# Indexer tiles of the first half in the first pass, x in reverse, weight sums that hold a block, and a planner rate of 360 GB/s

## The chip, the cores and the metric

The kernel runs on one core of one Trainium2 chip. The metric is the device time of one execution in microseconds; of several runs the median counts. A core has a matrix engine (TensorE, "PE", with its weight loads "PEld"), VectorE ("DVE"), ScalarE ("ACT"), GpSimd ("POOL") and SyncE ("SP"), which issues nearly all DMA transfers of this kernel.

## The reference, cut to what matters

One layer over a sequence of 1024 tokens, model width 2048. One input projection, 6752 columns wide, feeds two groups: sparse attention with a token indexer, and a Mamba-2 state-space mixer. One output projection and a layer norm follow.

```python
u = jnp.einsum('bsd,de->bse', h, w_in[layer])
q, k, v, z_attn, q_idx, k_idx, w_idx, z_ssd, xbc, dt_raw = _split_cols(u, IN_WIDTHS)
...
logits = jax.nn.relu(jnp.einsum('bqhd,bsd->bqhs', qib, k_idx32))      # 16 indexer heads of 64
score = jnp.einsum('bqhs,bqh->bqs', logits, wb)
score = jnp.where(admissible[None], score, -jnp.inf)                  # chunk-causal, chunks of 64
_, sel = lax.top_k(score, topk)                                       # 256 keys for each query
...                                                                   # softmax attention over those keys
mixed = jnp.concatenate([o_attn, o_ssd], axis=-1)
sub = jnp.einsum('bse,ed->bsd', mixed, w_out[layer])
h = _layer_norm(DEEPNORM_ALPHA * h + sub, ln_g[layer], ln_b[layer])
```

The first 256 queries have no more than 256 admissible keys, so the first half of the sequence needs indexer scores only for its last 256 queries (blocks 2 and 3 of 128), the second half for all 512 (blocks 4 to 7).

## The kernel before, in words

**Precision and pieces.** Each fp32 operand is split into a high and a low fp32r part (ScalarE copies the high part, VectorE subtracts: `w_split`, `t_xst`), and a product is three matmuls: high x high, high x low, low x high. The sequence has two halves of 512 tokens (h = 0, 1), the model width two halves of 1024 (u = 0, 1). A piece of the input projection (`Piece`, `emit_t`) multiplies one weight tile of 1024 x 128 by one "set" of x, that is one half h and one width half u, [8 x 128] x 512: 24 matmuls. Indexer tiles ("qi") of h = 0 use only the last 256 columns.

**The plan.** `PLAN` orders the input projection. A tuple (h, tiles, end) is a plain pass: each tile is multiplied by both sets of that half, u = 0 then u = 1. The first three tiles go together (u = 0 for all, then u = 1), then single tiles, then the last `end` tiles together. A list is a group: pairs of tiles go through a Winograd-Strassen scheme with seven products in four phases, over seven sets: x (1,0), the formed sums M2 and M3, x (0,1), the sums S1 and S4, and x (1,1). Sixteen buffers `xh` and sixteen `xl` hold two sets at once. In `units`, a set is requested (`request`, `t_xst`: four DMAs of 512 KB, eight splits) one piece before the set that is two places ahead of it in order of release has had its last use. Before, the order is: pass of h = 0 (5 tiles); pass of h = 1 (13 tiles, all its indexer tiles among them); first group (keys, values, queries); pass of h = 0 over its eight indexer tiles; second group (the rest of the state-space inputs and both gates).

**Tasks.** Everything behind a piece is a Python generator with a priority. `t_qi` rotates an indexer tile, splits it and makes score matmuls for two heads; `t_score` applies ReLU and adds the weighted logits. When all scores of a half are there (`ev_score`), `t_topk` finds the 256th largest by bit-wise search: 32 rounds of ScalarE sign-and-count and three small VectorE operations, for the blocks (2, 3), (4, 5) and (6, 7). Attention (`t_kv`, `t_attn`) runs in the order second half, first half; it needs the masks, and its tiles of the state-space part (`t_ssd`) and the gates run between the pieces. `t_wsum` forms the Strassen sums T1 to T4 of the output weights in DRAM, at priority 5. `t_xform` forms M2, M3, S1 and S4 of x in DRAM.

**The planner.** `Sim` is a model of the engines and of one DMA pipe (`Sim.dma`, L287 and on). At build time it decides which task is emitted next, and so the order of instructions on every queue: a task is emitted when its inputs, by the model, are there, its buffers are free and the clocks of its engines are not too far ahead of TensorE's. All engines then run their queues in that order. `spare_u` is the reserve of `u` buffers that tasks with `keep` leave free. Every instruction goes through one helper, so the profile gives all of them line L313; tiles are told apart by tag: `xt` x in DRAM, `xfM` and `xfS` the formed sums, `xr` and `s` raw x, `wr`, `wh`, `wl` raw, high and low weights, `wo` output weights, `ts` their sums, `pj`, `a`, `o` PSUM tiles, `u` working tiles, `q`, `mask` and `mx` DRAM scratch.

**The output projection** follows as seven products (A11, S3, S1, S2, A22, S4, A12, each eight pieces) over the mixed activations; `forms` and `t_form` load and add their operands. S3 needs the attention outputs of both halves.

Of the kernel before, what the change touches and what calls it, by code (L numbers as in the profile page):

```python
# [13 lines left out]
ALU = mybir.AluOpType  # L14

D = 2048
S = 1024
HALF = 512
P = 128
# [22 lines left out]
def tile_order():  # L42
# [10 lines left out]
FIRST = [("misc", 0), ("xbc", (0, 0)), ("xbc", (0, 1))]  # L53
KVQ = [("k", 0), ("k", 1), ("v", 0), ("v", 1)] + [("q", n) for n in range(8)]
QI = [("qi", j) for j in range(8)]
PLAN = [
    (0, FIRST + [("xbc", (0, 2)), ("xbc", (0, 3))], 2),
    (1, [("misc", 0)] + QI + [("xbc", (0, j)) for j in range(4)], 3),
    [(("k", 0), ("k", 1)), (("v", 0), ("v", 1))] + [(("q", n), ("q", n + 4)) for n in range(4)],
    (0, QI, 3),  # L60
    [(("xbc", (1, j)), ("xbc", (3, j))) for j in range(4)] + [(("xbc", (2, j)), ("xbc", (2, 2 + j))) for j in range(2)]
    + [(("zs", (n // 2, n % 2)), ("z", n)) for n in range(8)],
]
# [60 lines left out]
def in_dram(x):  # L124
    return "DRAM" in str(x.space)
# [6 lines left out]
class Sim:  # L132
# [154 lines left out]
    def dma(self, eng, out, in_, kw):  # L287
        q = {"SP": "SP", "A": "AQ", "G": "G"}[eng]
        lanes = self.lanes["G" if q == "G" else "H"]
        at, notes = self.deps([out], [in_], "D")  # L290
        start = max(self.clk[q], at, lanes.pop(0))
        issue = 1000.0 if eng == "G" else 350.0
        self.clk[q] = start + issue
        sb = in_ if in_dram(out) else out
        row = max(sb.ap[-1][1] * 4, 64)
        x = max(start + issue, self.clk["D"])
        self.clk["D"] = x + max(out.size(), in_.size()) * 4 * (1 / 400 + 0.6 / row)
        cell = [self.clk["D"] + self.LAND, start]
        lanes.append(cell[0])
        self.note(notes, cell, "D")  # L300
        return cell
# [268 lines left out]
class Layer:  # L570
# [20 lines left out]
    def units(self):  # L591

        pieces, work = [], []
        self.hooks = {}
        self.sets = []

        def put(p, listed=True):
            if listed:
                work.append((len(pieces), None))
            pieces.append(p)  # L600
            return len(pieces) - 1

        def plain(h, tile, u, n):
            kind, j = tile
            t = ORDER.index(tile)
            p = Piece("T", h, t, u, load=(("w", t, u),), n=n + u, open=u == 0, close=u == 1, key=(h, t),
                      s0=256 if (kind == "qi" and h == 0) else 0)
            if u == 1:
                p.done = lambda ps: self.fl.add(getattr(self, "t_" + kind)(h, j, ps), 0, f"{kind}{j}h{h}", self.fl.t + 100)
            put(p)  # L610

        for pairs in PLAN:
            if isinstance(pairs, tuple):
                h, tiles, end = pairs
                n = len(self.sets)
                self.sets += [("x", h, 0), ("x", h, 1)]
                for part in [tiles[:3]] + [[t] for t in tiles[3:-end]] + [tiles[-end:]]:
                    for u in range(2):
                        for tile in part:
                            plain(h, tile, u, n)  # L620
                continue
            gi = GROUPS.index(pairs)
            a11 = len(self.sets)
            base = a11 + 1
            self.sets += [("x", 1, 0), ("f", "M2"), ("f", "M3"), ("x", 0, 1), ("f", "S1"), ("f", "S4"), ("x", 1, 1)]
            n = [(a11, base), (base + 1, base + 2), (base + 3, base + 4)]
            couples = [list(range(c, min(c + 2, len(pairs)))) for c in range(0, len(pairs), 2)]
            if len(couples[-1]) == 1:
                couples[-2:] = [couples[-2] + couples[-1]]
            for ph in range(3):  # L630
                for couple in couples:
                    for f in range(2):
                        for c in couple:
                            i = put(self.product(gi, c, pairs[c], ph, f, n[ph][f]))
                            if ph and not (ph == 1 and f == 1):
                                self.hooks.setdefault(max(i - 1, 0), []).append(lambda gi=gi, c=c, ph=ph, f=f: self.pre_ld(gi, c, ph, f))
            for c in range(len(pairs)):
                i = put(self.product(gi, c, pairs[c], 3, 0, base + 5))
                self.hooks.setdefault(i - 1, []).append(lambda gi=gi, c=c: self.pre_ld(gi, c, 3, 0))
        end = {}  # L640
        for i, p in enumerate(pieces):
            end[p.n] = i
        for i in end.values():
            pieces[i].last = True
        freed = sorted(end, key=end.get)
        for n in range(2, len(self.sets)):
            at = end[freed[n - 2]] - 1
            self.hooks.setdefault(at, []).append(lambda n=n: self.request(n))
        self.n_t = len(pieces)
        self.hooks.setdefault(self.n_t - 6, []).append(lambda: self.forms(0))  # L650
        self.hooks.setdefault(12, []).append(self.form_tasks)
        for half in range(2):
            self.hooks.setdefault(12, []).append(lambda half=half: self.fl.add(self.t_wsum(half), 5, "wsum"))
        for n in range(7):
            for d in range(2):
                for j in range(4):
                    if n < 6 or 4 * d + j < 8 - SKEW:
                        work.append((len(pieces), (0, 1, 2, 3)))
                    name = PRODUCTS[n][1]
                    pieces.append(Piece("O", n, d, j, load=(("o", name, d, j),)))  # L660
        for sts in ((0,), (1,), (2,), (3,)):
            work += [(len(pieces) - SKEW + j, sts) for j in range(SKEW)]
        return pieces, work
# [150 lines left out]
    def t_wsum(self, half):  # L814

        fl = self.fl
        cols = slice(512 * half, 512 * half + 512)

        def load(name, d, j):
            x = fl.new("us", [P, 512])  # L820
            fl.dma(x, self.w_block(name, d, j)[:, cols])
            return x

        def save(name, d, j, x):
            fl.dma(self.tsum[name, d, j][:, cols], x)
        for d in range(2):
            for j in range(4):
                yield Need("D", u=2, keep=6)
                x, y = load("B22", d, j), load("B12", d, j)
                yield Need("V")  # L830
                fl.two(x, x, y, ALU.subtract)
                yield Need("D", us=1)
                save("T3", d, j, x)
                fl.free(x)
                z = load("B11", d, j)
                yield Need("V")
                fl.two(y, y, z, ALU.subtract)
                fl.free(z)
                yield Need("D", us=1)
                save("T1", d, j, y)  # L840
                x = load("B22", d, j)
                yield Need("V")
                fl.two(x, x, y, ALU.subtract)
                fl.free(y)
                yield Need("D", us=1)
                save("T2", d, j, x)
                z = load("B21", d, j)
                yield Need("V")
                fl.two(z, x, z, ALU.subtract)
                fl.free(x)  # L850
                yield Need("")
                save("T4", d, j, z)
                fl.free(z)
                fl.signal(self.ev_wsum[half][4 * d + j])
# [641 lines left out]
    def t_score(self, h, i, kh, m, head, r):  # L1496
        fl = self.fl
        yield Need("A")
        fl.act(r[:, 0:m], r[:, 0:m], AF.Relu)
        yield Need("V")  # L1500
        sc = self.score[h][i][:, kh * HALF:kh * HALF + m]
        wcol = getattr(self, f"sd{h}")["wsc"][:, (i - 4 * h) * 16 + head:(i - 4 * h) * 16 + head + 1]
        if head not in self.seen.setdefault((h, i, kh), set()) and not self.seen[h, i, kh]:
            fl.ts(sc, r[:, 0:m], wcol, 0.0, ALU.mult, ALU.add)
        else:
            fl.stt(sc, r[:, 0:m], wcol, sc, ALU.mult, ALU.add)
        self.seen[h, i, kh].add(head)
        fl.free(r)
        self.nlog[h] += 1
        if self.nlog[h] == (32 if h == 0 else 128):  # L1510
            fl.signal(self.ev_score[h])
            if h == 1:
                fl.free(*self.kk[1])
            else:
                fl.free(*self.kk[0])
                fl.spare_u = 4

# [770 lines left out]
```

## Time and profile before

| | |
|---|---|
| median of 3 runs | 1729.61 us (1725.16 to 1730.37) |
| the profiled execution | 1725.14 us, span of its instructions 1723.4 us |
| TensorE busy | 1638.7 us (95%), 8044 matmuls recorded |
| VectorE, ScalarE, GpSimd busy | 1353.0 us (79%), 1019.6 us (59%), 173.5 us (10%) |
| granted TensorE clock, mean | 0.986 |
| DMA | 446.50 MB, mean 259 GB/s |
| `xr<-xt` and `s<-xt`, 512 KB each | 28 and 28 transfers |

Matmuls are pipelined, so a matmul's recorded duration is longer than the distance to the next one; distances between starts are read from the timeline. A wait in square brackets stands behind the instruction that ended it, with what released it. A wait of several causes is put down to the last one.

### The profile page before, as it was taken

To read this page: it belongs to the slowest core of one execution; us is meant where nothing else is said; L and a number is where in the kernel's file an instruction comes from. 1 tells how busy PE (TensorE), PEld (TensorE's weight loads), DVE (VectorE), ACT (ScalarE), POOL (GpSimd) and SP (SyncE) were. 2 spreads that over 40 slices of the span, in tenths; PEclk is the share of its full clock that TensorE was granted. 3 is DMA by queue.
4 is the path that set the end of the run, shared out by engine and by line. 5 is a ranking of instruction groups with operands and counts; after the bars stand their busy time and mean duration, and the time that the engine had idled before them with its cause. 6 is when DMAs were issued, how large, how long until landed. Compare 5 with 4: busy or idle time off the path is not lost. (4 is left out here: it accounts for less than half of the span.)

```text
span 1723.4 us, 24378 instructions
## 1 busy us (share of the span) xinstructions
PE 1638.7 (95%) x8044; PEld 1351.2 (78%) x8044; DVE 1353.0 (79%) x2444; ACT 1019.6 (59%) x1799; POOL 173.5 (10%) x201
## 2 busy tenths in 40 slices
PE   9999999998887989999999999989999999999997
PEld 7877788876666978778888788877888877888875
DVE  5779999787567898789996788845777677659998
ACT  5745575678666856987555478456867544532320
POOL 0000010000000000000222111222121110000110
PEclk9999999999899999999999999999999999999998
DMA  9576578988787678989666875658778999877654
GB/s 320 202 253 230 198 258 290 324 310 307 246 294 259 222 266 271 315 299 318 227 220 219 312 236 188 220 186 251 241 230 280 313 314 342 298 278 268 218 193 147
DMA packets 210215, 446.50 MB, mean 259 GB/s; under 512 B 21928, under 2 KB 61992, under 8 KB 210088
## 3 DMA queue, kind: packets, MB, share of 16 engines
q1 hardware_dynamic: 209656, 444.55, 75.9%
q8 instruction: 63, 1.03, 0.2%
q14 instruction: 64, 0.52, 0.1%
q10 hardware_dynamic: 432, 0.39, 0.1%
HBM read 338.56 MB, written 106.30 MB: 258 GB/s over the span
## 5 line engine op out<-in xcount | busy, mean ns | idle before, releaser
L313 PE MATMUL pj<-xh,wh 128*128 128x512 f32 (+1 forms) x1192 | 470.0, 394 | 25.9 <-ACT wh L313 18.0
L313 PE MATMUL pj<-xh,wl 128*128 128x512 f32 (+1 forms) x1192 | 460.1, 386 | 9.3 <-DVE wl L313 9.1
L313 PE MATMUL pj<-xl,wh 128*128 128x512 f32 (+1 forms) x1192 | 458.8, 385 | 0.1
L313 DVE TENSOR_TENSOR wl<-wr,wh 128x1024 fp32r<-128x1024 f32 (+1 forms) x179 | 213.9, 1197 | 113.2 <-ACT wh L313 112.6
L313 PEld LDWEIGHTS pj<-xh,wh 128*128 128x128 f32 x1192 | 227.1, 191 | 70.7 <-ACT wh L313 20.6
L313 PEld LDWEIGHTS pj<-xh,wl 128*128 128x128 f32 x1192 | 226.5, 190 | 58.8 <-DVE wl L313 14.4
L313 PEld LDWEIGHTS pj<-xl,wh 128*128 128x128 f32 x1192 | 227.3, 191 | 41.2 <-DVE xl L313 1.8
L313 ACT ACTIVATE wh<-wr 128x1024 fp32r<-128x1024 f32 (+1 forms) x185 | 190.6, 1033 | 106.7 <-PE pj L313 67.2
L313 PE MATMUL pj<-xh,s 128*128 128x512 f32 (+1 forms) x688 | 222.1, 385 | 1.8 <-DVE u L313 1.6
L313 PE MATMUL a<-u,u 128*128 128x512 f32 (+3 forms) x746 | 171.7, 351 | 16.4 <-DVE u L313 7.0
L313 PEld LDWEIGHTS a<-u,u 128*128 128x128 f32 x746 | 123.3, 189 | 50.1 <-DVE s L313 10.6
L313 PEld LDWEIGHTS pj<-xh,s 128*128 128x128 f32 x688 | 127.7, 188 | 27.3 <-ACT xh L313 2.3
L313 DVE TENSOR_TENSOR u<-u,u 128x512 f32<-128x512 f32 (+7 forms) x212 | 130.2, 627 | 16.1 <-DMA u<-wo 4.5
L313 ACT ACTIVATE u<-s,sm 128x768 bf16<-128x768 f32 (+7 forms) x132 | 129.6, 982 | 21.3 <-DVE sm L313 19.5
L313 DVE TENSOR_TENSOR wr<-wr,wr 128x1024 f32<-128x1024 f32 (+1 forms) x98 | 121.6, 1243 | 20.5 <-DMA wr<-wt 19.4
L313 ACT ACTIVATE u<-a 128x512 fp32r<-128x512 f32 (+4 forms) x115 | 53.4, 479 | 138.0 <-DVE u L313 66.5
L313 PE MATMUL pj<-xl,s 128*128 128x512 f32 (+1 forms) x344 | 130.8, 380 | 0.8 <-DVE xl L313 0.8
L313 ACT ACTIVATE u<-u 128x512 f32<-128x512 f32 (+4 forms) x165 | 91.9, 566 | 61.5 <-DVE u L313 57.3
L313 ACT ACTIVATE a<-a 128x512 f32<-128x512 f32 (+3 forms) x160 | 76.1, 504 | 70.3 <-PE a L313 69.2
L313 DVE TENSOR_TENSOR s<-wr,s 128x1024 fp32r<-128x1024 f32 (+2 forms) x59 | 70.8, 1200 | 30.7 <-ACT s L313 30.5
L313 DVE TENSOR_TENSOR u<-pj,u 128x512 f32<-128x512 f32 (+2 forms) x94 | 62.4, 664 | 36.7 <-PE pj L313 31.0
L313 PE MATMUL pj<-wh,xh 128*128 128x512 f32 x218 | 87.8, 403 | 1.2 <-DVE u L313 1.2
(253 smaller groups left out, 2678.9 us busy)
## 6 DMA issues: line engine op xcount, KB each, us to landing
wr<-wt SPq DMA_DIRECT2D x228, 512.0 KB, 5.3
u<-u SPq DMA_DIRECT2D x100, 256.0 KB, 5.7
u<-wo SPq DMA_DIRECT2D x79, 256.0 KB, 5.1
wr<-ts SPq DMA_DIRECT2D x32, 512.0 KB, 5.7
ts<-u SPq DMA_DIRECT2D x63, 256.0 KB, 4.3
xr<-xt SPq DMA_DIRECT2D x28, 512.0 KB, 4.9
s<-xt SPq DMA_DIRECT2D x28, 512.0 KB, 6.6
u<-mx SPq DMA_DIRECT2D x49, 256.0 KB, 6.3
```

The source lines that it names most:

```text
L313: f(*args, **kw)
```

## The change

1. The eight indexer tiles of h = 0 stand at the end of the first pass, and the separate pass over them between the two groups is gone. `end` of the first pass is 3 instead of 2.
2. In the pass of h = 1, each tile uses the sets in the order u = 1, u = 0. The first group then begins with (1,0), which is resident, and does not request it again. The second group requests it as before.
3. The first pass's scores and top-k can come before those of the second half. The split keys of h = 0 are freed, and `spare_u` is set to 4, when the scores of both halves are counted (32 + 128 = 160).
4. `t_wsum` loads B22 once and writes T3 into a new buffer; its four subtractions are the same. It asks for three `u` buffers at its start instead of two.
5. The planner's DMA pipe moves 360 instead of 400 bytes per nanosecond.

```diff
 PLAN = [
-    (0, FIRST + [("xbc", (0, 2)), ("xbc", (0, 3))], 2),
+    (0, FIRST + [("xbc", (0, 2)), ("xbc", (0, 3))] + QI, 3),
     (1, [("misc", 0)] + QI + [("xbc", (0, j)) for j in range(4)], 3),
     [(("k", 0), ("k", 1)), (("v", 0), ("v", 1))] + [(("q", n), ("q", n + 4)) for n in range(4)],
-    (0, QI, 3),
...
-        self.clk["D"] = x + max(out.size(), in_.size()) * 4 * (1 / 400 + 0.6 / row)
+        self.clk["D"] = x + max(out.size(), in_.size()) * 4 * (1 / 360 + 0.6 / row)
...
-            p = Piece("T", h, t, u, load=(("w", t, u),), n=n + u, open=u == 0, close=u == 1, key=(h, t),
+            w = u if h == 0 else 1 - u
+            p = Piece("T", h, t, w, load=(("w", t, w),), n=n + u, open=u == 0, close=u == 1, key=(h, t),
...
-                self.sets += [("x", h, 0), ("x", h, 1)]
+                self.sets += [("x", h, h), ("x", h, 1 - h)]
...
             a11 = len(self.sets)
+            if self.sets[-1] == ("x", 1, 0):
+                a11 -= 1
+            else:
+                self.sets.append(("x", 1, 0))
             base = a11 + 1
-            self.sets += [("x", 1, 0), ("f", "M2"), ("f", "M3"), ("x", 0, 1), ("f", "S1"), ("f", "S4"), ("x", 1, 1)]
+            self.sets += [("f", "M2"), ("f", "M3"), ("x", 0, 1), ("f", "S1"), ("f", "S4"), ("x", 1, 1)]
...
-                yield Need("D", u=2, keep=6)
-                x, y = load("B22", d, j), load("B12", d, j)
+                yield Need("D", u=3, keep=6)
+                x, y, z = load("B22", d, j), load("B12", d, j), fl.new("us", [P, 512])
                 yield Need("V")
-                fl.two(x, x, y, ALU.subtract)
+                fl.two(z, x, y, ALU.subtract)
+                yield Need("")
+                save("T3", d, j, z)
+                fl.free(z)
                 yield Need("D", us=1)
-                save("T3", d, j, x)
-                fl.free(x)
                 z = load("B11", d, j)
                 yield Need("V")
                 fl.two(y, y, z, ALU.subtract)
                 fl.free(z)
+                fl.two(x, x, y, ALU.subtract)
                 yield Need("D", us=1)
                 save("T1", d, j, y)
-                x = load("B22", d, j)
-                yield Need("V")
-                fl.two(x, x, y, ALU.subtract)
                 fl.free(y)
-                yield Need("D", us=1)
                 save("T2", d, j, x)
...
             if h == 1:
                 fl.free(*self.kk[1])
-            else:
+            if sum(self.nlog) == 160:
                 fl.free(*self.kk[0])
                 fl.spare_u = 4
```

## The prediction

> **What bounds the kernel now.** I read the page's shares first, then busy time by stage, then the waits of TensorE, then the timeline around the longest one.
>
> ```profile
> span 1723.4 us, 24378 instructions
> PE 1638.7 (95%) x8044; PEld 1351.2 (78%) x8044; DVE 1353.0 (79%) x2444; ACT 1019.6 (59%) x1799; POOL 173.5 (10%) x201
> PEclk9999999999899999999999999999999999999998
> ```
> TensorE is busy 95% of the span, so what an order of work can win is its idle 1723.4 - 1638.7 = 84.7 us, and the time after a pause in which its clock is low. By stage (each row: PE, PEld, DVE, ACT, POOL busy us; granted clock, DMA share, GB/s):
>
> ```profile
> 70.00:246.00 176.00, 170.15 (x760) 136.82 (x759) 151.51 (x236) 96.65 (x173) 9.96 (x10) 0.99 0.65 227
> 246.00:390.00 144.00, 141.49 (x648) 115.89 (x647) 123.51 (x206) 94.60 (x168) 10.23 (x12) 1.00 0.89 309
> 390.00:546.00 156.00, 133.65 (x568) 104.51 (x567) 106.84 (x237) 109.29 (x200) 2.48 (x2) 0.95 0.82 284
> 546.00:650.00 104.00, 85.88 (x558) 77.23 (x557) 93.28 (x171) 70.02 (x117) 2.81 (x2) 0.95 0.69 239
> 650.00:1200.00 550.00, 536.20 (x2707) 445.77 (x2706) 426.90 (x842) 358.34 (x638) 83.35 (x84) 1.00 0.76 253
> 1340.00:1712.00 372.00, 364.04 (x1764) 299.72 (x1762) 294.65 (x461) 135.93 (x221) 31.77 (x24) 1.00 0.79 265
> ```
> The rows are: second pass; first and later part of the first group; the separate pass over the first half's indexer tiles with the start of the second group; the rest of the input projection; the output projection. Idle is 5.9, 2.5, 22.4, 18.1, 13.8 and 8.0 us. Two stretches of 260 us hold 40.5 of it and the low clock. The change takes the fourth stage out of its place and eases the data traffic of the third. What TensorE waits for in the third (first two rows) and the fourth stage (last two; us, times, longest), shorter waits left out:
>
> ```profile
> PE pj L313 <- ACT xh L313: 6.8, 2, 3.5
> PE pj L313 <- ACT wh L313: 5.8, 1, 5.8
> PE pj L313 <- ACT wh L313: 10.7, 2, 9.1
> PE pj L313 <- DVE wl L313: 4.1, 5, 1.6
> ```
>
> **Part 1: the indexer tiles move to the first pass.** The longest wait, in the timeline:
>
> ```profile
> 538.46 4.97 SPq L313 DMA_DIRECT2D xr<-xt  x2
> 545.10 1.04 SPq L313 DMA_DIRECT2D s<-xt  x2
> 546.62 0.28 PE L313 MATMUL pj<-xh,wh 128*128 128x256 f32 x1
> 549.37 0.28 PE L313 MATMUL pj<-xh,wl 128*128 128x256 f32 x1
> 555.34 2.41 ACT L313 ACTIVATE xh<-s 128x512 fp32r<-128x512 f32 x4 [3.89 <-DMA s<-xt]
> 557.65 1.99 ACT L313 ACTIVATE wh<-wr 128x1024 fp32r<-128x1024 f32 x2
> 558.74 0.58 PE L313 MATMUL pj<-xh,wh 128*128 128x256 f32 x1 [9.09 <-ACT wh L313]
> 563.80 0.32 PE L313 MATMUL pj<-xl,wh 128*128 128x256 f32 x1
> ```
> The first indexer piece runs 546.62 to 549.37, 2.75 us for 24 matmuls, 0.12 us each, since these tiles use only 256 query columns; a piece of 512 columns takes twice that, about 5.5 us (estimate). Its second piece needs the other half of x, which is only then arriving: ScalarE stands at 555.34 for the DMA, and the weight split queued behind it on ScalarE comes at 557.65. TensorE loses 9.1 us. Until 563.80 it does 19 matmuls in 5.06 us that take 19 x 0.12 = 2.3 us at full clock: 2.8 us more. In the first pass both halves of x are resident for all the tiles, so this wait has no counterpart: **-11.9 us**. By the Trainium skill ("TensorE: Matmul & The Clock Gate", Part 1) the half clock after a pause lasts one window of about 3.4 us, a loss of about 1.7 us, and this term would be -10.8 us; the row shows it longer here.
>
> What is late next: the second group no longer begins after short tiles. Its first x (second half, u=0) is asked for when the first group's last phase begins, whose 6 pieces cover it, and is then used through 2 pieces while M2 lands. The precedent of a swap right behind indexer tiles is the present one into the second group: DVE wl 4.1 us and one ACT wh wait of 1.6 us. In the new order that swap is first pass to second pass, with 3 short pieces and their scores as cover, and three long pieces for the other half: **+1 us** (between 0 and the 9.1 us above; nearest is the present swap's first wait, whose cover is the same three pieces).
>
> The work that moves, by its rows (DVE, and the top-k of the first half, which is allowed to start when its scores are done):
>
> ```profile
> L313 DVE TENSOR_TENSOR wl<-wr,wh 128x1024 fp32r<-128x1024 f32 x15 | 18.0, 1220 | 5.2 <-ACT wh L313 5.2
> L313 DVE TENSOR_TENSOR xl<-xr,xh 128x512 fp32r<-128x512 f32 x12 | 7.7, 685 | 1.9 <-ACT xh L313 1.9
> L313 DVE SCALAR_TENSOR_TENSOR u<-a,wsc,u 128x512 f32<-128x512 f32 x8 | 6.0, 745 | 0.2
> L313 DVE TENSOR_TENSOR u<-u,u 64x256 fp32r<-64x256 f32 x14 | 5.9, 420 | 0.4
> L313 DVE SCALAR_TENSOR_TENSOR u<-a,wsc,u 128x384 f32<-128x384 f32 x9 | 5.5, 613 | 0.5 <-ACT a L313 0.3
> L313 DVE STREAM_SHUFFLE u<-pj 128x256 f32<-128x256 f32 x7 | 3.1, 447 | 0.0
> L313 DVE TENSOR_TENSOR pj<-pj,u 128x256 f32<-128x256 f32 x7 | 3.0, 431 | 0.0
> L313 DVE TENSOR_SCALAR sm<-sm 128x2 f32<-128x2 f32 x52 | 9.0, 174 | 0.2
> ```
> One tile costs DVE 2 x 1.22 (weights) + 0.45 + 3 x 0.43 (rope) + 2 x 0.42 + 2 x (0.745 + 0.613) (scores) = 7.7 us; eight cost 62 us. TensorE needs 2 x 2.9 + about 1.5 us of score matmuls (estimate, eight at 0.12 to 0.23) = 7.3, or 58 us. So the tiles load DVE fully wherever they stand. The top-k adds 32 rounds of three small operations at about 0.17 us plus some 7 us of passes over the scores (estimate from the 384 and 512 wide rows above), 23 us. From 70 to 390 DVE was busy 275 of 320 us (86%) and TensorE idle 8.4 us. With the move it is 275 + 62 + 23 - 5.5 (8 splits of x, 0.685 each, that the first group's resident x saves here) = 354 of 378 us, 94%. Nearest rows: the four 50-us slices from 100 to 300,
>
> ```profile
> 100.00:150.00 50.00, 44.61 (x194) 35.07 (x193) 44.48 (x76) 24.32 (x47) 1.39 (x3) 0.97 0.61 212
> 250.00:300.00 50.00, 50.00 (x228) 41.32 (x227) 46.98 (x64) 29.73 (x51) 5.02 (x4) 1.00 0.85 296
> ```
> (first and last of four) have DVE near 93% with TensorE idle 5.9 us, 3%; the fourth stage has DVE at 90% and idle 18.1 - 9.1 = 9.0 us beside the wait above, 9%. At 3% the 378 us lose 11 us, at 9% 33 us; the old places lost 8.4 + 9.0 = 17 us. So this term lies between -6 and +16. I take **-5**: the same place, other work of low priority there (weight sums, the state-space task) that can go later, and the same DVE share.
>
> **Part 2: x in reverse, three sets fewer.**
>
> ```profile
> xr<-xt SPq DMA_DIRECT2D x28, 512.0 KB, 4.9
> s<-xt SPq DMA_DIRECT2D x28, 512.0 KB, 6.6
> u<-wo SPq DMA_DIRECT2D x79, 256.0 KB, 5.1
> ```
> Gone are the two sets of the separate pass and the reload of (second half, u=0): 12 transfers of 512 KB and their issues on SP, 24 splits on DVE (0.685, 16 us) and on ACT (2.41 us for four in the timeline above, 15 us). The first group's start shows no wait to win (246 to 390: 2.5 us idle), so beside Part 1 this is **0**; if its cover fails, it costs one wait like the 3.5 us for xh above.
>
> **Parts 3 and 4: weight sums hold B22; 360 GB/s; buffers.** 16 loads of 256 KB go, the 64 vector operations stay. Each sum now asks for three buffers at its start, so it can start later; nothing uses the sums before the output projection. The key buffers come free when both halves' scores are done, after which the reserve held back from the sums falls to 4: earlier than now, which lets sums into the first group. With the 360 the planner throttles them more. In the third stage TensorE loses 22.4 us to splits behind late x; bounds are -22 (all gone) and +9 (one more wait like the longest). Of the 4 MB saved about a quarter falls here (estimate), 2% of the 284 GB/s x 156 us = 44 MB moved, and the rate is the unknown. I take **-2**. What the queue does when full:
>
> ```profile
> 600.00:610.00 10.00, 9.18 (x74) 8.89 (x74) 9.67 (x21) 7.57 (x14) 0.00 (x0) 1.00 1.02 404
> 1340.00:1480.00 140.00, 136.28 (x718) 111.49 (x717) 96.48 (x171) 67.36 (x131) 10.89 (x8) 1.00 0.98 326
> ```
> 326 GB/s over 140 full microseconds, 404 at best: 360 is nearer the long row than 400. The Trainium skill ("HBM Reference", Specifications (TRN2)) has a lone core at about 425 GB/s, against this edit; by that the term would be 0, not -2.
>
> **Sum.** -11.9 + 1 - 5 + 0 - 2 = -18 us. The profiled run took 1725.1 us for a span of 1723.4; that gives 1707. It stands 4.5 us under the median 1729.6, so the same gain from the median is 1712; I say 1709.
>
> **The rivals.** *Vector work moves the loss along.* Part 1's third term at +16 instead of -5: 1707 + 21 = 1728, no change. For: DVE at 94%; against: 3% idle at 93% today.
>
> *Attention comes late, slower.*
>
> ```profile
> 323.12 0.82 ACT L313 ACTIVATE u<-s,sm 128x640 bf16<-128x640 int16 x1
> 664.03 0.38 SPq L313 DMA_DIRECT2D mask<-u  x1
> 712.45 1.83 SPq L313 DMA_DIRECT2D u<-q  x2
> 1321.48 1.44 SPq L313 DMA_DIRECT2D o<-u  x1
> ```
> Top-k of the second half begins at 323 when its scores are done; its second mask is stored at 664, attention starts at 712 and ends at 1321. The input projection ends near 1340, and the product S3, which needs the last attention output, comes 8 pieces of 5.5 us later. In the new order scores end 58 us later, with the first half's top-k up to 81. If all that follows keeps its length, attention ends at 1379 to 1402 while S3 wants it at 1340 - 18 + 44 = 1366: 13 to 36 us idle, 1720 to 1743; I take the upper half, 1738. Attention lasts 1321 - 712 = 609 us, so this decides once it starts after 1366 - 609 = 757. Against: the moved stage itself, with DVE full, lies between 546 and 650, in the last part of that top-k, and would be gone from there.
>
> *The planner's rate does the more.* With 360 the third stage's waits halve, -11 instead of -2: 1698.
>
> **Chances.** Forecast 0.56 (its own range 1695 to 1721), vector work 0.23, late attention 0.17, rate 0.04. A change under 0.3% (5 us) can't be told from none here. Faster: 0.55 + 0.05 + 0.04 = 0.64; same: 0.01 + 0.15 + 0.03 = 0.19; slower: 0.03 + 0.14 = 0.17. The range takes the bounds of the DVE term and part of the third stage's: 1692 to 1735.
>
> **What would show it.** Right: no wait above 4 us between the first group's last phase and the second group's first; 128x256 projection matmuls between about 65 and 130 us; 44 xt transfers of 512 KB, 64 u<-wo, about 436 MB; DVE near 1337 us; TensorE's busy time unchanged and its idle near 69 us. Wrong: DVE full with TensorE idle above 14 us between 65 and 390; first u<-q after 757 us with a wait at the start of the output projection; the first group's waits longer than 22 us.

## The result and the profile after

| | before | after |
|---|---|---|
| median | 1729.99 us (1725.16 to 1731.27, 4 runs) | 1743.34 us (1741.14 to 1745.16, 4 runs) |
| ratio | | 1.0090, 95% interval 1.0066 to 1.0114 |
| profiled execution, span, mean granted clock | 1725.14 us, 1723.4 us, 0.986 | 1744.33 us, 1742.5 us, 0.976 |

The forecast was 1709 us; it came 13 us longer than before. The first lines of the page of the changed kernel:

```profile
span 1742.5 us, 24238 instructions
PE 1655.5 (95%) x8044; PEld 1361.3 (78%) x8044; DVE 1349.8 (77%) x2427; ACT 1008.7 (58%) x1774; POOL 158.1 (9%) x194
PEclk9999999999999979999999999999999999999999
```

TensorE's idle time is 1742.5 - 1655.5 = 87.0 us where it was 84.7. The 16.8 us more of busy time are the same 8044 matmuls at a lower clock: one slice of the 40 shows a 7 (the fifteenth, 610 to 653 us), where none of before is under 8.

Where it went is seen when both executions are cut at the same places of the program: the start of the second group (its first `t<-wr`, the store of a weight sum that SP issues), the last such store, which ends the second group's first phase, and the first matmul of the output projection. First the four stages of before, then the four of after (columns: stretch, its length; PE, PEld, DVE, ACT, POOL busy and instructions; granted clock, DMA share, GB/s):

```profile
0.00:615.30 615.30, 568.03 (x2687) 463.32 (x2688) 489.63 (x873) 400.96 (x699) 30.41 (x48) 0.98 0.76 267
615.30:779.50 164.20, 156.97 (x722) 126.83 (x722) 136.35 (x301) 125.09 (x258) 3.17 (x5) 1.00 0.83 284
779.50:1359.60 580.10, 569.22 (x2973) 477.76 (x2972) 438.57 (x820) 364.02 (x631) 108.21 (x124) 1.00 0.74 244
1359.60:1711.40 351.80, 344.39 (x1668) 283.33 (x1666) 280.50 (x438) 129.55 (x212) 30.75 (x23) 1.00 0.78 261
```

```profile
0.00:597.60 597.60, 574.16 (x2715) 466.12 (x2716) 487.94 (x889) 381.44 (x701) 18.07 (x40) 0.99 0.69 241
597.60:794.80 197.20, 167.60 (x711) 132.53 (x710) 137.04 (x309) 149.99 (x277) 12.58 (x10) 0.90 0.80 269
794.80:1376.80 582.00, 576.03 (x3068) 486.00 (x3066) 451.36 (x813) 355.56 (x611) 101.84 (x125) 1.00 0.76 254
1376.80:1730.60 353.80, 337.70 (x1556) 276.68 (x1554) 265.57 (x405) 121.67 (x187) 24.62 (x18) 0.97 0.76 252
```

When the second group starts, the changed kernel is 615.3 - 597.6 = 17.7 us ahead: by that place a gain of the forecast size has arrived, with TensorE idle 23.4 us up to there instead of 47.3. The next stage then takes 33.0 us more with 11 matmuls fewer: idle 29.6 us instead of 7.2, and a clock of 0.90 instead of 1.00. The third stage is 1.9 us longer (with 95 matmuls more), the output projection 2.0 us. -17.7 + 33.0 + 1.9 + 2.0 = +19.2 us; the spans differ by 19.1.

TensorE's waits for high halves of weights in the long stage, first before (615 to 779.5 us), then after (598 to 795 us; us, times, longest), and the two longest of them in the timeline of after:

```profile
PE pj L313 <- ACT wh L313: 1.6, 1, 1.6
PE pj L312 <- ACT wh L312: 24.4, 7, 5.4
630.86 0.79 PE L312 MATMUL pj<-xh,wh 128*128 128x512 f32 x1 [5.40 <-ACT wh L312]
722.33 0.79 PE L312 MATMUL pj<-xh,wh 128*128 128x512 f32 x1 [4.44 <-ACT wh L312]
```

The matmuls of the same stage by the name of their weight buffer, first two groups of before (616 to 779.5), then two of after (last column: idle just before them and what ended it):

```profile
L313 PE MATMUL pj<-xh,wh 128*128 128x512 f32 x134 | 52.7, 394 | 1.6 <-ACT wh L313 1.6
L313 PE MATMUL pj<-xh,s 128*128 128x512 f32 x112 | 37.5, 396 | 0.1
```

```profile
L312 PE MATMUL pj<-xh,wh 128*128 128x512 f32 x163 | 70.6, 433 | 27.4 <-ACT wh L312 24.4 <-ACT xh L312 3.0
L312 PE MATMUL pj<-xh,s 128*128 128x512 f32 x58 | 18.7, 393 | 0.0
```

TensorE waits for high halves of weights (`wh`) that ScalarE has not split yet. There are two `wh` buffers; when both are taken, `w_split` puts a high half into a free `s` buffer, and for those TensorE hardly ever waits. Before fed 112 of these matmuls from `s`, after only 58. Lines from ScalarE's queue at the start of the stage (brackets: idle time before the line, and what ended it):

```profile
603.22 1.15 ACT L312 ACTIVATE xh<-xr 128x512 fp32r<-128x512 f32 x2 [12.05 <-DMA xr<-xfM]
625.59 0.82 ACT L312 ACTIVATE u<-s,sm 128x640 bf16<-128x640 f32 x1
626.54 0.94 ACT L312 ACTIVATE u<-s,sm 128x768 bf16<-128x768 f32 x1
627.47 1.03 ACT L312 ACTIVATE u<-s,sm 128x896 bf16<-128x896 int16 x1
628.62 1.15 ACT L312 ACTIVATE u<-s,sm 128x1024 bf16<-128x1024 int16 x1
629.77 1.04 ACT L312 ACTIVATE wh<-wr 128x1024 fp32r<-128x1024 f32 x1
```

It stands 12.05 us for the second group's M2, and then the sign rounds (`u<-s,sm`) of the second half's two top-k tasks lie between the weight splits: four of them, from 625.59 on, go ahead of the split at 629.77 that ended TensorE's wait of 5.40 us. Those rounds are here because the first half's top-k now goes first; e3 below, where it goes later, has them elsewhere. Before had no 640-wide round between 600 and 700 us, after 17.

### The profile page after: what moved, and what is told of

Its sections match the earlier page's. It is cut to its first block, busy times and chain, and to the rows that moved or that the text cites. A ratio compares the mean times of both kernels' runs of the same rounds, so it can differ in the third digit from the quotient of the medians.

```text
span 1742.5 us, 24238 instructions
## 1 busy us (share of the span) xinstructions
PE 1655.5 (95%) x8044; PEld 1361.3 (78%) x8044; DVE 1349.8 (77%) x2427; ACT 1008.7 (58%) x1774; POOL 158.1 (9%) x194
## 5 line engine op out<-in xcount | busy, mean ns | idle before, releaser
L312 PE MATMUL pj<-xh,wh 128*128 128x512 f32 (+1 forms) x1144 | 454.2, 397 | 37.2 <-ACT wh L312 26.2
L312 PE MATMUL pj<-xh,wl 128*128 128x512 f32 (+1 forms) x1144 | 445.2, 389 | 4.4 <-DVE wl L312 4.3
L312 PE MATMUL pj<-xl,wh 128*128 128x512 f32 (+1 forms) x1144 | 443.3, 388 | 0.2 <-DVE xl L312 0.2
L312 PE MATMUL pj<-xh,s 128*128 128x512 f32 (+1 forms) x784 | 253.2, 385 | 0.1
L312 PEld LDWEIGHTS pj<-xh,s 128*128 128x128 f32 x784 | 146.1, 189 | 28.6 <-issue 1.1
L312 PE MATMUL pj<-xl,s 128*128 128x512 f32 (+1 forms) x392 | 149.6, 382 | 0.8 <-DVE xl L312 0.8
L312 ACT ACTIVATE u<-s,sm 128x896 bf16<-128x896 int16 (+7 forms) x132 | 129.9, 984 | 25.4 <-DVE sm L312 23.5
L312 DVE TENSOR_TENSOR wr<-wr,wr 128x1024 f32<-128x1024 f32 x98 | 120.8, 1236 | 19.7 <-DMA wr<-wt 18.7
L312 PE MATMUL pj<-s,xh 128*128 128x512 f32 x260 | 85.7, 400 | 1.9 <-ACT xh L312 1.7
L312 PEld LDWEIGHTS pj<-xl,s 128*128 128x128 f32 x392 | 74.1, 189 | 13.9 <-DVE xl L312 1.2
```

The costliest lines, as they stand in the source:

```text
L312: f(*args, **kw)
```

## The experiments

Eighteen kernels ran. In one kind the planner draws a new order of instructions (whole kernels). In the other the planner is told the full operation and the chip gets less of it, so that every remaining instruction keeps its place in every queue ("fixed order"). Ratios are against before, which ran again beside each batch (medians 1724.8 to 1727.6 us), with 95% intervals; they differ from the quotients of the medians by up to 0.0014. A difference of 0.001 is 1.7 us. What is read from a trace is from one execution of each kernel.

**Which part does it?** The first three are the changed kernel with one thing undone, the next three before with one part alone.

```diff
-(1 / 360 + 0.6 / row)                                     # e1: after, the rate undone
+(1 / 400 + 0.6 / row)
...
-    (0, FIRST + [("xbc", (0, 2)), ("xbc", (0, 3))] + QI, 3),   # e2: after, Part 1 undone
+    (0, FIRST + [("xbc", (0, 2)), ("xbc", (0, 3))], 2),
...
+    (0, QI, 3),
...
-        yield Need("G", ev=(self.ev_score[h],))            # e3: after, first half's top-k after masks 4, 5
+        yield Need("G", ev=(self.ev_score[h],) + ((self.ev_msk[4], self.ev_msk[5]) if h == 0 else ()))
```

> The changed kernel with the planner's DMA pipe back at 400. Theory A (the moved indexer tiles push the second half's scores and top-k later, from 323 to 460 us, so that its ScalarE rounds stand over the start of the second group): the rate matters little, 1738 to 1748 us, with the first wide sign round of the second half still after 430 us. Theory B (the rate: the planner emits sums and loads at other places, and TensorE's weight splits come late): back to 1722 to 1732 us.

Measured: 1746.13 us, 1.0112 (1.0086 to 1.0137). Without the rate the loss stays, though in this order the second group's first phase is shorter than in the changed kernel: 180.0 us, with 14.0 us of waits for `wh`.

> The changed kernel with the first half's indexer tiles back in their own pass between the groups; x in reverse, held B22 and 360 stay. Theory A: the loss is gone, 1720 to 1732 us, top-k of the second half from about 320 us. Theory B: the loss stays, 1738 to 1748 us.

Measured: 1748.00 us, 1.0115 (1.0093 to 1.0137). The loss stays without the moved tiles, but it is spread in another way: the second group starts at 624.5 us, 9 us later than in before, and its first phase takes 183.9 us, with 11.3 us of waits for `wh`, not 24.4.

> The changed kernel, but the first half's top-k waits until the masks of blocks 4 and 5 are stored. Theory A in the form that this top-k is what pushes the second half's back: the second half's first wide sign round comes before 420 us and the time falls to 1725 to 1735 us. In the form that the scores and rope of the moved tiles on VectorE push it: still after 430 us, 1738 to 1748 us. Theory B: 1740 to 1748 us.

Measured: 1747.91 us, 1.0127 (1.0108 to 1.0145). With the 640-wide rounds back at 383 to 624 us the phase still takes 201 us, with 24.6 us of waits for `wh`. So the place of that top-k alone does not decide either.

e4 is before with 360, e5 before with x in reverse (Part 2), e6 before with the weight sums that hold B22 (item 4 of the change), each alone; their edits are the hunks of the change above.

> The kernel before with only the planner's rate at 360. Theory A: within 5 us of 1730. Theory B: 1738 us or more.

Measured: 1734.74 us, 1.0045 (1.0030 to 1.0060).

> The kernel before with only x in reverse (the first group begins with resident x; the indexer pass stays). Theory D (one of the small parts costs 10 us or more by itself): 1738 us or more here or with the held B22 alone. Theory A (the loss is made at the second group's start, by the moved tiles): 1722 to 1732 us here. Theory C (any new order of emission moves the time by some 10 us, with nothing gained or lost in work): anywhere from 1722 to 1745, with the change in waits of TensorE spread over stages that the edit does not touch.

Measured: 1745.70 us, 1.0113 (1.0077 to 1.0148).

> The kernel before with only the weight sums that hold B22 (16 loads of 256 KB fewer). Theory D: 1738 us or more here or with x in reverse. Theory A: 1722 to 1732 us. Theory C: anywhere from 1722 to 1745, with 4 MB less moved in either case.

Measured: 1749.05 us, 1.0123 (1.0090 to 1.0156). Each of these three parts alone makes before slower, although two of them only take work away. That fits a common cause: each draws a new order. The moved tiles alone in before were not run.

**What does a new order cost by itself?** e7, e8 (before) and e9, e10 (after) change a number that no engine sees, the time that the planner's model adds for a transfer to land:

```diff
-    LAND = 2500.0
+    LAND = 2520.0        # e7, e9; 2480.0 in e8, e10
```

> The kernel before with one number of the planner's model changed that stands for nothing on the chip: the landing time of a DMA 2520 instead of 2500 ns. Theories A and D: within 3 us of 1728, since no work and no order that they speak of changes. Theory C: moved by more than 5 us, in stages that have no reason to change.

Measured: 1754.31 us, 1.0166 (1.0132 to 1.0201).

> The same with 2480 ns. Theories A and D: within 3 us of 1728. Theory C: moved by more than 5 us here or with 2520.

Measured: 1759.84 us, 1.0190 (1.0162 to 1.0218). Twenty nanoseconds in the model, either way, cost before 28 and 33 us on the chip.

> The changed kernel with the planner's landing number 2520 in place of 2500 (nothing else; the chip never sees the number, only the order of emission that follows from it). Theory C (the time of a kernel of this planner hangs on the order drawn, and the order of before was a good draw): the change's own gain shows when both kernels are drawn again, so that this one stands below before with the same landing number (1754.31), as a draw around 1735 to 1750. Theory A (the change by itself delays the second half's scores and always makes its loss at the second group's start): this kernel stands 10 us or more above before with the same number, that is at 1764 or more.

Measured: 1741.16 us, 1.0081 (1.0060 to 1.0101).

> The changed kernel with the landing number 2480. Theory C: below before with the same number (1759.84), around 1735 to 1750. Theory A: at 1770 or more. If this one and the 2520 one fall on different sides of before with their numbers, then neither the change's sign nor its size can be read from single orders.

Measured: 1755.13 us, 1.0159 (1.0135 to 1.0183), 5 us above what Theory C gave it. Both lie under the 1764 and 1770 us of Theory A. At 2520 the changed kernel is the faster one by 0.0085, at 2480 by 0.0031 (the two intervals overlap), at 2500 the slower one by 0.0090. The three orders of before average 1.0119, those of after 1.0110. Over drawn orders the change is worth nothing that three draws can tell, and the order of before is an unusually good one: no other whole kernel here came within 0.4% of it.

Something of the change is the same in every order, though. In the seven whole kernels with the moved tiles (after, e1, e3, e9, e10, and e15 and e16 below) the second group starts at 597.3 to 604.7 us; in the seven without (before, e2, e4 to e8) at 607.6 to 637.0. TensorE's waits for `wh` in the second group's first phase are 14.0 to 30.8 us in the seven with, 0 to 11.3 us in those without. So the gain before the group and the longer waits at its start both go with the moved tiles. The length of the phase does not divide the two kinds: 180.0 to 201.1 us with, 157.4 to 197.8 without (e5 197.8, e7 197.2), and TensorE's idle time in it is 15.8 to 35.9 us with, 3.5 to 18.9 without.

**Is it M2, is it the sign rounds?** At fixed order, in the changed kernel (e11: M2; e13: rounds) and in before (e14).

```diff
-        fl.dma(raw, ...)                                   # e11: set 11; hi and lo are split from 64 columns broadcast
+        fl.nc.sync.engine.dma_start(raw[:, :, 0:64], full[:, :, 0:64])
...
-        fl.act(junk[:, 0:(i + 1) * P], src, AF.Sign, ...)  # e13, e14: h == 1 only
+        fl.nc.scalar.engine.activation(junk[:, 0:64], src[:, 0:64], AF.Sign, ...)
```

> The changed kernel with its instructions in the very same order on every engine, but the second group's M2 set is loaded with 64 of its 512 columns, and its halves are split from these 64 columns broadcast (its other columns are left out of the computation). If ScalarE's 12.05 us wait for that transfer at 603 us starts the loss at the second group's start (the waits for weight halves between 610 and 755 and the half clock): that wait goes down to under 3 us, TensorE's idle time between 600 and 770 falls from 29 us by 12 or more, and the time by 10 to 20 us, to 1723 to 1733. If the loss is the work queued on ScalarE and VectorE there, and the wait only overlapped it: the time falls by under 5 us.

Measured: 1740.15 us, 1.0076 (1.0057 to 1.0095), not told apart from the changed kernel. The edit did not do what it was for. ScalarE and TensorE in this kernel:

```profile
601.22 2.20 ACT L791 ACTIVATE xh<-xr 128x512 fp32r<-128x512 f32 x4 [11.17 <-DMA xr<-xfM]
627.38 0.79 PE L313 MATMUL pj<-xh,wh 128*128 128x512 f32 x1 [7.60 <-ACT wh L313]
```

With an eighth of the bytes the transfer landed hardly sooner: ScalarE still stood 11.17 us. What M2's wait is worth stays open.

> Before with its instructions in the very same order on every engine, but with the traffic that the change removes made nearly nothing: the three x sets (the second group's x (0,1), its M2, and x (0,1) of the indexer pass) are loaded with 64 of 512 columns and split from these broadcast, and the 16 second loads of B22 are left out (their subtraction takes another tile, so the sums are wrong). The forecast's removed wait (11.9 us before the second indexer piece) is a gain at a fixed order: 1729 less 10 to 14, 1715 to 1720. If the wait is made up for elsewhere (the work behind it waits for something else): 1725 to 1730.

This expectation names the sets wrongly: the three loads made thin are the removed ones, the first group's x (1,0) and both sets of the separate indexer pass. Measured: 1720.11 us, 0.9959 (0.9944 to 0.9974), 7 us shorter, where the expectation had 10 to 14. The wait that the prediction priced, in this kernel:

```profile
552.91 1.99 ACT L314 ACTIVATE wh<-wr 128x1024 fp32r<-128x1024 f32 x2
554.00 0.58 PE L314 MATMUL pj<-xh,wh 128*128 128x256 f32 x1 [6.38 <-ACT wh L314]
```

The wait falls from 9.09 to 6.38 us only, since the thin loads, too, came late (ScalarE waited 3.06 us for the last). The second group starts at 610.35 us, 4.9 earlier, and little is lost again behind it: its first phase takes 165.3 us, 1.1 more than in before. At a fixed order the removed traffic is a gain.

> The changed kernel with its instructions in the very same order on every engine, but the 132 sign rounds of the second half's two top-k lanes on ScalarE run on 64 columns each (the masks of the second half come out wrong; all other work is whole). Theory A2: the change moved these rounds into the second group's first stage (28 of its 640- and 896-wide rounds lie in 600 to 700 us, 4 before), where the weight splits queue behind them in order. Then TensorE's waits for weight halves between 598 and 795 us fall from 24.4 to under 8 us, the clock there rises from 0.90 to above 0.95, and the time falls by 20 us or more, to 1713 to 1724. Rival M (the stage starves because the weights' transfers or VectorE's halves come late, and ScalarE's rounds only lie beside it): the time falls by less than 8 us.

Measured: 1733.20 us, 1.0059 (1.0042 to 1.0077). ScalarE's busy time in the phase falls from 150.0 to 97.6 us, but the phase only from 197.2 to 190.4, and TensorE's waits for `wh` to 17.0. Theory A2 had asked for under 8.

> The same on before, whose sign rounds lie elsewhere: (4,5) at 323 to 578 us, (6,7) at 347 to 759. Theory A2: little of that is on the path, the time falls by 0 to 8 us, to 1720 to 1729. If it falls by as much as the changed kernel does, the rounds cost the same wherever they lie, and the move of them is not the cause of the difference.

Measured: 1721.15 us, 0.9978 (0.9965 to 0.9990). So the length of the rounds costs the changed kernel 5 us and before 4: where they lie makes no difference that these runs can tell.

**Both away, and the waits between the rounds.** e17 (after) and e18 (before), still at fixed order, leave out the second half's sign rounds and the VectorE steps between them, and load the second group's M2 thin.

```diff
-        fl.act(junk[:, 0:(i + 1) * P], src, AF.Sign, ...)   # h == 1 only
-        fl.tt(...); fl.ts(...); fl.stt(...)                 # the three steps of a round
```

> The changed kernel with every other instruction in its order on every engine: the second half's 128 sign rounds on ScalarE and the 192 small VectorE steps behind them are left out (so ScalarE no longer waits for VectorE between rounds), and the second group's M2 is loaded with 64 of 512 columns. The masks of the second half and the sums with M2 come out wrong. Theory A2 with M2 (these two together are what makes the second group's first stage long): the stage, 197 us, comes to 170 us or less, and the time 20 us or more below the changed kernel's, to a ratio of 0.997 or less of before. Rival O (the new order itself: with the long work gone, other waits in the queues that are served in order come in its place): ratio 1.001 to 1.006, the stage 180 us or more.

> The same two left out of before, in its order. Theory A2 with M2: little, ratio 0.994 to 1.000, so that the two kernels stand within 5 us of each other once the rounds and M2 are out. Rival O: the two kernels keep most of their distance, 8 us or more.

Measured: 1727.23 us, 0.9997 (0.9979 to 1.0015), and 1715.64 us, 0.9942 (0.9925 to 0.9960). The change's distance goes from 0.0090 to 0.0055, from 15.5 to 9.5 us (by the medians from 13.4 to 11.6). The phase takes 183.1 us against 161.5: 14.1 us less than in the changed kernel, and 2.7 us less than in before. So the rounds with their waits look like a part of the loss, though the fall of the distance is not clear of the intervals; most of the distance stays, as rival O said, though e17 lies between the two forecasts (M2's wait on ScalarE was still 10.46 us). What is left is seen in the timeline of e17, from which nearly all of ScalarE's rounds for the second half are gone (first PE, then ACT lines):

```profile
707.38 0.39 PE L313 MATMUL pj<-xh,wl 128*128 128x512 f32 x1
709.40 0.50 PE L313 MATMUL pj<-xh,wh 128*128 128x512 f32 x1 [1.63 <-ACT wh L313]
710.66 0.50 PE L313 MATMUL pj<-xh,wl 128*128 128x512 f32 x1 [0.53 <-DVE wl L313]
...
707.81 0.60 ACT L313 ACTIVATE u<-pj 128x512 f32<-128x512 f32 x1 [2.57 <-PE pj L313]
708.30 2.00 ACT L313 ACTIVATE wh<-wr 128x1024 fp32r<-128x1024 f32 x2
```

ScalarE was free, and waited 2.57 us for TensorE to end the piece; it copied the result out and split the next two weights; and for these TensorE waited 1.63 us. Two engines that serve their queues in order pass the wait to and fro. Waits for `wh` of 1.6 to 1.9 us behind such a copy-out stand at 632.0, 671.5, 682.4, 709.4 and 737.9; at 606.6 and 622.3 (1.72 and 2.80 us) ScalarE had itself waited for a weight sum of VectorE. Here only 61 of the `pj<-xh` matmuls took weights from `s`. Before breaks this up in two ways that the order gives it: more splits ahead in `s`, and other matmuls between two pieces. That these two are what breaks it up is read from the traces and was not tested. Of tile `a` (scores and state-space products), in 102 us from the start of the phase, first before, then after (columns as above, without POOL):

```profile
616.00:718.00 102.00, 14.78 (x60) 10.21 (x60) 20.09 (x33) 12.51 (x26) 1.00 0.81 272
598.00:700.00 102.00, 5.45 (x26) 4.62 (x26) 4.20 (x10) 0.81 (x3) 0.87 0.77 263
```

48 of the 60 are the first half's scores, which the change has moved to the first pass.

Over all orders, matmuls `pj<-xh` from `s` in the phase and us of waits for `wh`: before 112 and 1.6; e6 112, 1.1; e8 112, 8.5; e4 96, 10.2; e5 80, 4.8; e7 80, none; e1 64, 14.0; e9 59, 25.0; after 58, 24.4; e2 50, 11.3; e15 48, 19.1; e10 48, 30.8; e3 48, 24.6; e16 32, 18.2. On the whole, where fewer splits run ahead TensorE waits longer, but not strictly: e16 has the fewest and waits less than e10. Why fewer do is argued and not shown: the second half's scores lie in `s` buffers (`t_score`) until their masks are made, and before stored the first of these at 587 and 664 us, after at 693 and 703. An order with the same top-k and more `s` buffers was not tried.

**A version without the loss?** e15 keeps the top-k of blocks (6, 7) behind masks 4 and 5, so that two sign lanes instead of four lie at the group's start; e16 draws its order again (`LAND = 2520.0`).

```diff
-        yield Need("G", ev=(self.ev_score[h],))
+        yield Need("G", ev=(self.ev_score[h],) + ((self.ev_msk[4], self.ev_msk[5]) if blocks[0] == 6 else ()))
```

> The changed kernel, whole, where the (6,7) lane of the second half's top-k waits until the masks (4,5) are done, so that two lanes instead of four lie in the second group's first stage; the planner draws a new order. Theory A2: waits for weight halves in that stage under 15 us instead of 24.4, the third run of stores earlier by 10 us or more, and the time 1725 to 1740; below 1727 it would beat before. Against it: the masks (6,7) come near 900 us, and if attention needs them earlier the loss comes back there, 1740 or more.

> The kernel of the run before this one with the landing number 2520: a second draw of its order, to tell what the waiting lane does from what the draw does. Theory A2: 1725 to 1740 again, and below the changed kernel with the same number (1741.16). If the two stand more than 12 us apart, the edit's own worth can't be read from either.

Measured: 1740.70 us, 1.0106 (1.0084 to 1.0128), and 1745.22 us, 1.0126 (1.0111 to 1.0141). The waits for `wh` fall to 19.1 and 18.2 us, where Theory A2 had asked for under 15; the phase still takes 194.2 and 199.7 us. No whole kernel here beats before.

## Why the prediction was wrong, step by step

**The longest wait, -11.9, and what lies ahead of the second group.** The wait is gone as forecast, and the marker stands where it should:

```profile
65.17 0.28 PE L312 MATMUL pj<-xh,wh 128*128 128x256 f32 x1
123.49 0.28 PE L312 MATMUL pj<-xh,wl 128*128 128x256 f32 x1
196.79 0.77 PE L312 MATMUL pj<-xh,wh 128*128 128x512 f32 x1 [5.54 <-DVE u L312]
```

5.54 us is the longest wait up to the second group. From 65 to 390 us TensorE is idle 11.9 us, under the 14 named as a sign against, and VectorE is busy 88%: the vector-work rival did not come. The terms ahead of the second group together are right in size, -17.7 of -18. That it is so near is partly luck of the two orders: with the moved tiles the group starts 10.6 to 18.0 us ahead of before (604.7 to 597.3 against 615.3), and other orders of before start it at 607.6 to 637.0. How the 17.7 us divide among the terms no run shows. For the removed traffic alone e12 has 4.9 us up to this place, at a fixed order and with the wait shortened only from 9.09 to 6.38. Of the 2.8 us that the prediction counted as slow matmuls after the wait, 0.46 are a second wait, for a low half at 560.00.

**"What is late next": the step that failed.** The prediction looked for the new wait at the swap of x: "whose 6 pieces cover it, and is then used through 2 pieces while M2 lands". It gave no term to the second group's first phase. M2 came 12.05 us late for ScalarE, and the weight splits behind it in that queue were not asked about at all. In the changed kernel this phase was +33.0 us, where the sum had nothing: +22.4 us of idle time (7.2 us before), 24.4 us of waits for weight halves (1.6 before), and a clock of 0.90 (1.00 before). How much of it M2's lateness is worth alone stays open, and so does why fewer splits run ahead. The indexer tiles were more than a place with a 9 us wait: their scores gave TensorE other work in that phase (60 matmuls in 102 us, after 26), and the earlier end of the second half's top-k went with more weight splits ahead in `s`. The move was priced at its old place and at its new one, but not for what the old place did for its neighbours. The sign named against it, a wait above 4 us at that place, is there twice in the second group's first phase: 5.40 us at 630.86 and 4.44 at 722.33.

**The DVE term and Part 2, Part 4.** The counts are as forecast: `xr<-xt` and `s<-xt` 16 + 28 = 44 transfers, 64 `u<-wo`:

```profile
DMA packets 206183, 436.01 MB, mean 250 GB/s; under 512 B 21480, under 2 KB 61544, under 8 KB 206056
u<-wo SPq DMA_DIRECT2D x64, 256.0 KB
xr<-xt SPq DMA_DIRECT2D x16, 512.0 KB
s<-xt SPq DMA_DIRECT2D x28, 512.0 KB
```

VectorE is busy 1349.8 us, not near 1337, and TensorE's busy time grew by 16.8 us where no change was forecast.

**Late attention.** The rival that ended slower had the sign right and the place wrong. The first `u<-q` comes at 745.20 us, before the 757 from which it decides, and the last `o<-u` at 1277.83, earlier than the 1321.48 of before:

```profile
745.20 0.92 SPq L312 DMA_DIRECT2D u<-q  x2
1277.83 0.37 SPq L312 DMA_DIRECT2D o<-u  x1
1438.82 0.79 PE L312 MATMUL a<-wh,xh 128*128 128x512 f32 x1 [9.77 <-DVE u L312]
```

The wait of 9.77 us in the output projection (its idle time is 16.1 us, before 7.4) is for VectorE's operands; with 112 matmuls fewer to do there, the stage is 2.0 us longer all the same.

**The planner's rate.** Taken back in the changed kernel it gives 1.0112, put into before 1.0045: neither way a gain.

**What no term had.** A sum of edits against one execution supposes that the rest keeps its order. Here every edit lets the planner draw another one, and the draws of before lie 0 to 33 us above the one shown. A range of 1692 to 1735 was too narrow by that alone; the shown time was the lowest of its kind.

## What to carry to other kernels

Where a planner at build time orders queues that are served in order, ask what else a moved block did in its old place: which engine had work between two pieces, and which buffers it let others fill ahead. Price an edit at a fixed order (tell the planner the whole operation and run less) and then draw the order several times with a number that means nothing: a difference below the spread of those draws belongs to the draw. A wait that goes at one end can come back where the next queue was only just in time, and cutting the profile at the same places of the program shows that at once.

## What was not expected of the hardware

Short waits can cost clock too. In e17 the clock is full when a wait of 1.63 us ends at 709.40 and one of 0.53 us at 710.66. The matmuls of 711.00 and 711.23 still start 0.23 us apart, as at full clock; the next ones 0.37 and 0.42 us apart:

```profile
711.00 0.40 PE L313 MATMUL pj<-xh,wh 128*128 128x512 f32 x1
711.23 0.57 PE L313 MATMUL pj<-xl,wh 128*128 128x512 f32 x1
711.60 0.63 PE L313 MATMUL pj<-xh,wl 128*128 128x512 f32 x1
712.02 1.91 PE L313 MATMUL a<-u,u 128*128 128x128 f32 x8
715.61 0.39 PE L313 MATMUL pj<-xl,wh 128*128 128x512 f32 x1
```

The granted clock microsecond by microsecond (third column from the end):

```profile
710.00:711.00 1.00, 0.47 (x3) 0.30 (x3) 1.00 (x2) 1.00 (x2) 0.00 (x0) 1.00 1.07 410
711.00:712.00 1.00, 1.00 (x4) 0.78 (x3) 1.00 (x2) 0.25 (x1) 0.00 (x0) 0.65 1.08 406
712.00:713.00 1.00, 1.00 (x6) 0.97 (x5) 1.00 (x2) 0.00 (x0) 0.00 (x0) 0.50 0.90 315
713.00:714.00 1.00, 1.00 (x7) 0.78 (x7) 1.00 (x1) 0.48 (x1) 0.00 (x0) 0.50 1.03 395
714.00:715.00 1.00, 1.00 (x14) 1.00 (x16) 0.83 (x3) 0.15 (x1) 0.00 (x0) 0.65 0.57 219
715.00:716.00 1.00, 1.00 (x11) 0.74 (x6) 1.00 (x3) 0.00 (x0) 0.00 (x0) 1.00 1.08 406
```

At half clock for 0.7 + 1 + 1 + 0.7 = 3.4 us, TensorE, which does not pause in that time, loses 1.7 us. The Trainium skill ("TensorE: Matmul & The Clock Gate", Part 1) has the clock go down after an idle window of about 3.4 us. Here two pauses of 1.63 and 0.53 us were enough, and the measurement decides. It does not happen each time: the same pair of pauses at 632.04 and 633.29 left the clock at 1.00, and so did 1.63 and 1.59 us at 638.58 and 640.91 in before; what decides is not shown. The phase of the changed kernel, with seven waits of 1.8 to 5.4 us spread over it, ran at 0.90, and about 17 us of the whole kernel's loss are the clock's (busy time 1655.5 against 1638.7).

A transfer made eight times smaller was not much sooner there. The second group's M2 in e11 (64 KB each), issued from 589.21 us, let ScalarE go on at 601.22; with 512 KB each, issued from 590.25, at 603.22: 12.0 and 13.0 us.
